# Weights that begin 16 bytes inside their tiles: a kernel whose matmuls run back to back, and the addresses they read

## The chip, the core and the metric

The kernel runs on one core of one Trainium2 chip. A core has five engines that run side by side and meet at semaphores: TensorE (PE in the profile, its weight loads PEld), VectorE (DVE), ScalarE (ACT), GpSimd (POOL) and SyncE (SP, which issues most DMAs here). The metric is device microseconds of one execution, the median of several runs.

## What is computed

Two transformer blocks on 256 tokens of width 1024, all in float32. The first has two layers (a sparse attention with compressed, selected and windowed keys; then a dilated attention), each followed by a SwiGLU feed-forward of 2816 hidden channels. The second has a feed-forward, a mixer of three branches (indexed sparse attention, a state-space scan, attention over a memory), and another feed-forward. There are so four feed-forwards:

```python
def swiglu(h, w_up, w_down):
    a, b = jnp.split(h @ w_up, 2, axis=-1)
    return (jax.nn.silu(a) * b) @ w_down
...
x = x + swiglu(rmsnorm(x, norm_ffn[layer]), ffn_w_up[layer], ffn_w_down[layer])
```

Most of the work is products of the activations with weight matrices that are read once from HBM.

## The kernel before

**Three products for one.** TensorE multiplies in a faster float32 form (F32R) that keeps fewer bits. So each operand is split into a rounded half h and the rest l, and a product is the sum of three: h with h, l with h, h with l. `mm3` (lines 223 to 230) issues them one after another into one PSUM bank: line 228 streams the activations' h against the weights' h, line 229 the activations' l against the weights' h, line 230 the activations' h against the weights' l. The activations move (128 partitions x 256 tokens), the weights are stationary (128x128). Every matmul has its own weight load.

**The path of a weight.** `load` (line 174) brings 128 x 2048 elements, 1 MB, into a `raw` tile by a DMA from SyncE's queue; `split` (line 181) makes of each 1024 columns a tile wh on ScalarE (line 187) and a tile wl on VectorE (line 188); four buffers of each. `units` (line 191) deals them out in pieces of 128 columns, 512 bytes. The activations are split the same way into tiles xh and xl in xs_pool (eight k-tiles, h and l, two buffers each), and the hidden channels of a feed-forward into hh and hl in a pool of its own.

**What sets the order.** A scheduler of the framework orders the instructions as it builds the program, by priorities and its own timeline. The projections take PSUM banks in turn (mm, sc, tr, ov: `take`, line 235). In a feed-forward the up projection is 44 units of eight k-tiles, 44 x 8 x 3 = 1056 matmuls in a row; the down projection follows with 8 units of 22 k-tiles of hidden channels, 528 matmuls.

**Where the tiles lie.** The pools are laid out in SBUF one after another, in bytes of each partition's row, tiles on multiples of 32: const, xres, a pad of 192, xs_pool (32 tiles of 1024 bytes), a pad of 320 (line 131), raw (4 x 8192), wsp (4 tiles wh and then 4 tiles wl, 4096 each), tmp (7360 bytes), then what a stage opens. So from the first tile of xs_pool to the first of the weights it is 32 x 1024 + 320 + 4 x 8192 = 65,856 bytes, which is 64 modulo 128 (320 modulo 512); all tiles and pieces in between are multiples of 512 bytes apart, so this holds for each pair of a piece of weights and a moving tile of xs_pool. From the first of the weights to the first hidden tile hh it is 8 x 4096 + 7360 + 4096 = 44,224 bytes in the first feed-forward; in the second 13,472 of a pool "late" and a pad of 320 come on top (58,016), in the third another 2112 (60,128), in the fourth the pad is 416 (58,112). Weights minus moving tile is thus 64, 96, 32 and 0 modulo 128 in the four down projections.

Of the kernel before, what the change touches and what calls it, by code (L numbers as in the profile page):

```python
# [12 lines left out]
F32R = mybir.dt.float32r  # L13
# [5 lines left out]
P = 128  # L19
# [102 lines left out]
class Builder:  # L122
    def __init__(self, ctx, tc, A):
        self.ctx, self.tc, self.nc, self.A = ctx, tc, tc.nc, A
        nc = self.nc
        e = ctx.enter_context
        self.cpool = e(tc.tile_pool(name="const", bufs=1))
        self.xpool = e(tc.tile_pool(name="xres", bufs=1))
        self.pad(e(tc.tile_pool(name="pad0", bufs=1)), 192)
        self.xs_pool = e(tc.tile_pool(name="xsplit", bufs=2))  # L130
        self.pad(e(tc.tile_pool(name="pad1", bufs=1)), 320)
        self.raw = e(tc.tile_pool(name="raw", bufs=4))
        self.wsp = e(tc.tile_pool(name="wsplit", bufs=4))
        self.tmp = e(tc.tile_pool(name="tmp", bufs=2))
        self.mm = e(tc.tile_pool(name="mm", bufs=2, space=PSUM))
        self.sc = e(tc.tile_pool(name="sc", bufs=2, space=PSUM))
        self.tr = e(tc.tile_pool(name="tr", bufs=2, space=PSUM))
        self.ov = e(tc.tile_pool(name="ov", bufs=2, space=PSUM))
        self.uid = 0
        self.turn = 0  # L140
        self.wide = True

        self.vec = self.cpool.tile([P, NVEC], F32, name="vec")
        self.gains = self.cpool.tile([P, KD * len(GAINS)], F32, name="gains")
        nc.scalar.dma_start(self.gains, A["vec"][:, :KD * len(GAINS)])
        self.con = self.cpool.tile([P, NCON], F32, name="con")
        self.ident = self.con[:, COFF["ident"]:COFF["ident"] + P]
        self.ones = self.cpool.tile([P, P], F32, name="ones")
        nc.vector.memset(self.ones, 1.0)
        self.mhalf = self.cpool.tile([P, 16], F32, name="mhalf")  # L150
        nc.gpsimd.memset(self.mhalf, -0.5)

        for _ in range(WARM):
            nc.tensor.matmul(self.bank("mm")[:, :P], self.ones, self.ones, start=True, stop=True)
# [25 lines left out]

    def split(self, v, kb, cols):
        nc = self.nc
        h = self.wsp.tile([P, 1024], F32R, tag="wh", name=self.n("wh"))
        l = self.wsp.tile([P, 1024], F32R, tag="wl", name=self.n("wl"))
        hv = h[:, :kb * cols].rearrange("p (k c) -> p k c", c=cols)
        lv = l[:, :kb * cols].rearrange("p (k c) -> p k c", c=cols)
        nc.scalar.activation(hv, v, AF.Copy)  # L187
        nc.vector.tensor_tensor(lv, v, hv.bitcast(F32), ALU.subtract)  # L188
        return [(hv[:, k], lv[:, k]) for k in range(kb)]
# [1243 lines left out]
```

## Time and profile before

| | |
|---|---|
| median of 3 runs | 1356.58 us (1354.99 to 1357.75) |
| profiled execution | 1361.28 us, its span 1359.3 us |
| TensorE busy | 1333.4 us, 98% of the span |
| VectorE busy | 999.9 us, 74% |
| ScalarE busy | 747.5 us, 55% |
| DMA queue of SyncE | 226 MB, 52.5% of the 16 engines' span |
| granted TensorE clock, mean | 0.995 |

The span is the time from the first to the last instruction of one profiled execution. Matmuls are pipelined: each is listed with about 0.28 us, but the next starts long before that is over, so the distance from start to start says how fast they go. In the view of busy time by stretch a row has the stretch and its length, then for PE, PEld, VectorE, ScalarE and GpSimd the busy time and, in brackets, the number of instructions that ran in the stretch, also those that had begun before it; then TensorE's granted clock (1.00 is full speed), the DMA engines' busy share and GB/s. The feed-forwards lie at about 170 to 346 us, 593 to 748, 798 to 949 and 1168 to 1346, the up projection first in each.

### The profile page before, as it was taken

How to read it: one execution, taken by the hardware profiler on the slowest of the kernel's cores; microseconds unless marked ns; L12 is line 12 of the kernel's file. 1: busy time of each engine (PE TensorE's matmuls, PEld its weight loads, DVE VectorE, ACT ScalarE, POOL GpSimd, SP SyncE). 2: the span in 40 equal slices, each digit the busy share in tenths (PEclk: the TensorE clock that was granted, in tenths of full speed). 3: DMA queues.
4: the chain of work that ended last, by engine and by line, in shares of the span. 5: the costliest groups of instructions: out<-in, count | busy, mean ns of one | idle time of the engine just before them, and what ended most of it. 6: DMA issues, size and time to landing. Idle time of an engine off the chain costs nothing.

```text
span 1359.3 us, 27471 instructions
## 1 busy us (share of the span) xinstructions
PE 1333.4 (98%) x10944; PEld 1266.8 (93%) x10944; DVE 999.9 (74%) x2087; ACT 747.5 (55%) x1414; POOL 188.7 (14%) x225
## 2 busy tenths in 40 slices
PE   8999999999999999999999999999999999999997
PEld 7786999999998887899999999999988879999997
DVE  6899677766697673998954877765699888777643
ACT  4677555545568785754544555544434665554442
POOL 4300100001210000422100310001032044000011
PEclk9999999999999999999999999999999999999998
DMA  9851365545865350456756466655754254655451
GB/s 280 251 160 63 109 198 188 188 142 188 247 202 182 114 139 9 147 191 216 233 182 201 154 207 201 194 187 157 243 162 148 79 170 158 199 186 189 152 193 43
DMA packets 227120, 232.77 MB, mean 171 GB/s; under 512 B 5944, under 2 KB 221184, under 8 KB 226992
## 3 DMA queue, kind: packets, MB, share of 16 engines
q1 hardware_dynamic: 223392, 226.14, 52.5%
q10 hardware_dynamic: 3600, 4.88, 1.0%
q8 instruction: 86, 1.41, 0.4%
q14 instruction: 42, 0.34, 0.1%
HBM read 226.69 MB, written 4.30 MB: 170 GB/s over the span
## 4 chain that ended last, share of the span: by engine, by line
PE 88%; DVE 6%; DMA 2%; issue 2%; ACT 1%; POOL 0%; SPq 0%; POOLq 0%; DVEq 0%; ACTq 0%
PE mm L228 11%; PE mm L229 11%; PE mm L230 11%; PE tr L230 6%; PE sc L230 6%; PE tr L228 6%; PE tr L229 6%; PE sc L228 6%; PE sc L229 6%; PE ov L473 3%; PE ov L228 3%; PE ov L230 3%; PE ov L229 3%; PE sc L777 2%; DVE wl L188 2%
## 5 line engine op out<-in xcount | busy, mean ns | idle before, releaser
L187 ACT ACTIVATE wh<-raw 128x1024 fp32r<-128x1024 f32 (+2 forms) x405 | 417.9, 1036 | 447.1 <-PE mm L229 141.7
L188 DVE TENSOR_TENSOR wl<-raw,wh 128x1024 fp32r<-128x1024 f32 (+2 forms) x405 | 489.9, 1212 | 167.9 <-ACT wh L187 163.1
L228 PE MATMUL mm<-xh,wh 128*128 128x256 f32 x952 | 272.5, 286 | 2.5 <-ACT wh L187 2.5
L230 PE MATMUL mm<-xh,wl 128*128 128x256 f32 x952 | 269.1, 283 | 1.0 <-DVE wl L188 1.0
L229 PE MATMUL mm<-xl,wh 128*128 128x256 f32 x952 | 269.4, 283 | 0.0
L228 PEld LDWEIGHTS mm<-xh,wh 128*128 128x128 f32 x952 | 180.8, 190 | 10.0 <-issue 4.7
L229 PEld LDWEIGHTS mm<-xl,wh 128*128 128x128 f32 x952 | 180.6, 190 | 4.3 <-issue 4.1
L230 PEld LDWEIGHTS mm<-xh,wl 128*128 128x128 f32 x952 | 179.8, 189 | 3.5 <-issue 1.6
L293 POOL TENSOR_TENSOR sqacc<-sqacc,sq 128x256 f32<-128x256 f32 x60 | 62.3, 1040 | 605.1 <-ACT sq L292 328.5
L228 PE MATMUL sc<-xh,wh 128*128 128x256 f32 x464 | 130.2, 281 | 1.8 <-ACT wh L187 1.8
L229 PE MATMUL sc<-xl,wh 128*128 128x256 f32 x464 | 130.0, 280 | 0.0
L230 PE MATMUL sc<-xh,wl 128*128 128x256 f32 x464 | 129.9, 280 | 0.0
L230 PE MATMUL tr<-xh,wl 128*128 128x256 f32 x440 | 123.2, 280 | 0.0
L229 PE MATMUL tr<-xl,wh 128*128 128x256 f32 x440 | 123.1, 280 | 0.0
L228 PE MATMUL tr<-xh,wh 128*128 128x256 f32 x440 | 123.1, 280 | 0.0
L228 PEld LDWEIGHTS sc<-xh,wh 128*128 128x128 f32 x464 | 88.0, 190 | 2.0 <-ACT wh L187 2.0
L229 PEld LDWEIGHTS sc<-xl,wh 128*128 128x128 f32 x464 | 87.6, 189 | 0.0
L230 PEld LDWEIGHTS sc<-xh,wl 128*128 128x128 f32 x464 | 87.2, 188 | 0.0
L228 PEld LDWEIGHTS tr<-xh,wh 128*128 128x128 f32 x440 | 83.4, 189 | 0.0
L229 PEld LDWEIGHTS tr<-xl,wh 128*128 128x128 f32 x440 | 83.0, 189 | 0.0
L230 PEld LDWEIGHTS tr<-xh,wl 128*128 128x128 f32 x440 | 82.7, 188 | 0.0
L228 PE MATMUL ov<-xh,wh 128*128 128x256 f32 x224 | 62.9, 281 | 0.0
(475 smaller groups left out, 3401.3 us busy)
## 6 DMA issues: line engine op xcount, KB each, us to landing
raw<-in_ffn_w_up_dram SPq DMA_DIRECT2D x44, 1024.0 KB, 5.3
raw<-in_ffn_w_in_dram SPq DMA_DIRECT2D x44, 1024.0 KB, 5.3
raw<-in_w_in_dram SPq DMA_DIRECT2D x17, 1024.0 KB, 5.2
raw<-in_ffn_w_down_dram SPq DMA_DIRECT2D x16, 1024.0 KB, 5.3
raw<-in_ffn_w_out_dram SPq DMA_DIRECT2D x16, 1024.0 KB, 5.3
raw<-in_b_w_q_dram SPq DMA_DIRECT2D x12, 1024.0 KB, 5.2
raw<-in_a_w_in_dram SPq DMA_DIRECT2D x8, 1024.0 KB, 8.7
bt<-u_scratch SPq DMA_DIRECT2D x28, 256.0 KB, 4.8
```

Source lines behind the costliest of these rows:

```text
L187: nc.scalar.activation(hv, v, AF.Copy)
L188: nc.vector.tensor_tensor(lv, v, hv.bitcast(F32), ALU.subtract)
L228: nc.tensor.matmul(ps, sh, mh, start=(i == 0), stop=False)
L229: nc.tensor.matmul(ps, sh, ml, start=False, stop=False)
L230: nc.tensor.matmul(ps, sl, mh, start=False, stop=(i == n - 1))
L293: nc.gpsimd.tensor_tensor(acc[:, 0], acc[:, 0], s, ALU.add)
L473: nc.tensor.matmul(O[64 * i:64 * i + 64, q0:q1], V[kb], pt[:, c0:c0 + q1 - q0], start=(start and kb == 0), stop=(stop and kb == 1), skip_g ...
L777: nc.tensor.matmul(ps, Q[d, h][:, qb * P:qb * P + P], K[d][g], start=(i == 0), stop=(i == 1))
```

## The change

Inside `split`, the tiles wh and wl become 1056 elements wide, and the kernel uses the elements 4 to 1027 of them, so that the weights begin 16 bytes inside the tile. The pad ahead of raw goes from 320 to 32 bytes. Nothing else changes: apart from that pad's memset, each engine has the same instructions in the same order.

```diff
-        self.pad(e(tc.tile_pool(name="pad1", bufs=1)), 320)
+        self.pad(e(tc.tile_pool(name="pad1", bufs=1)), 32)
...
     def split(self, v, kb, cols):
         nc = self.nc
-        h = self.wsp.tile([P, 1024], F32R, tag="wh", name=self.n("wh"))
-        l = self.wsp.tile([P, 1024], F32R, tag="wl", name=self.n("wl"))
+
+        h = self.wsp.tile([P, 1056], F32R, tag="wh", name=self.n("wh"))[:, 4:1028]
+        l = self.wsp.tile([P, 1056], F32R, tag="wl", name=self.n("wl"))[:, 4:1028]
         hv = h[:, :kb * cols].rearrange("p (k c) -> p k c", c=cols)
         lv = l[:, :kb * cols].rearrange("p (k c) -> p k c", c=cols)
```

From the first tile of xs_pool to the first weights it is now 32 x 1024 + 32 + 4 x 8192 + 16 = 65,584 bytes, 48 modulo 128. The buffers of a weight tile are 4224 bytes apart instead of 4096. The hidden tiles move with the pools: raw and the weights' tiles start 288 bytes lower, tmp and what follows 736 bytes higher.

## Rows read from the trace of the kernel before

**Rows 1.** Parts 1 and 4 of the page: busy us (share of the span) xinstructions; the chain.

```profile
PE 1333.4 (98%) x10944; PEld 1266.8 (93%) x10944; DVE 999.9 (74%) x2087; ACT 747.5 (55%) x1414; POOL 188.7 (14%) x225
...
PE 88%; DVE 6%; DMA 2%; issue 2%; ACT 1%; POOL 0%; SPq 0%; POOLq 0%; DVEq 0%; ACTq 0%
```

**Rows 2.** Busy time by stretch, all engines: stretch, length, busy us (xinstructions) per engine; clock.

```profile
180.00:280.00 100.00, 100.00 (x851) 100.00 (x850) 71.85 (x107) 50.40 (x71) 0.00 (x0) 1.00 0.56 183
292.00:342.00 50.00, 50.00 (x427) 50.00 (x426) 32.08 (x38) 25.30 (x37) 5.03 (x5) 1.00 0.60 198
600.00:685.00 85.00, 85.00 (x724) 85.00 (x723) 77.70 (x180) 43.06 (x62) 15.46 (x24) 1.00 0.69 220
692.00:745.00 53.00, 53.00 (x449) 53.00 (x448) 26.25 (x28) 22.54 (x28) 4.35 (x3) 1.00 0.62 203
802.00:882.00 80.00, 80.00 (x709) 80.00 (x708) 61.57 (x94) 43.52 (x63) 0.00 (x0) 1.00 0.61 194
892.00:942.00 50.00, 50.00 (x424) 50.00 (x424) 29.05 (x32) 23.19 (x32) 5.09 (x5) 1.00 0.58 188
1172.00:1282.00 110.00, 110.00 (x937) 110.00 (x936) 79.49 (x120) 56.30 (x82) 0.00 (x0) 1.00 0.58 190
1290.00:1340.00 50.00, 50.00 (x419) 50.00 (x419) 24.04 (x26) 20.49 (x25) 7.04 (x5) 1.00 0.46 149
```

**Rows 3.** Order of time, TensorE, second up projection: start us, length us, line, out<-in.

```profile
649.84 0.28 PE L228 MATMUL mm<-xh,wh 128*128 128x256 f32 x1
649.96 0.28 PE L229 MATMUL mm<-xl,wh 128*128 128x256 f32 x1
650.08 0.28 PE L230 MATMUL mm<-xh,wl 128*128 128x256 f32 x1
650.20 0.28 PE L228 MATMUL mm<-xh,wh 128*128 128x256 f32 x1
```

**Rows 4.** Order of time, TensorE, third up projection.

```profile
849.79 0.28 PE L228 MATMUL ov<-xh,wh 128*128 128x256 f32 x1
849.91 0.28 PE L229 MATMUL ov<-xl,wh 128*128 128x256 f32 x1
850.02 0.28 PE L230 MATMUL ov<-xh,wl 128*128 128x256 f32 x1
850.13 0.28 PE L228 MATMUL ov<-xh,wh 128*128 128x256 f32 x1
```

**Rows 5.** Order of time, the norm's sums ahead of the third up projection.

```profile
764.15 1.86 PEld L299 LDWEIGHTS ov<-ones,sqacc 128*128 128x128 f32 x16
...
764.26 1.84 PE L299 MATMUL ov<-ones,sqacc 128*128 128x1 f32 x16
```

**Rows 6.** Line 228's own matmuls by output bank: xcount, duration ns min/median/max, first and last start.

```profile
L228 PE MATMUL mm<-xh,wh x952: 276/281/684, 9.1 to 1282.5; 128*128 128x256 f32 x191
...
L228 PE MATMUL sc<-xh,wh x464: 276/281/385, 14.9 to 1285.3; 128*128 128x256 f32 x155
...
L228 PE MATMUL tr<-xh,wh x440: 276/281/364, 24.8 to 1276.8; 128*128 128x256 f32 x147
...
L228 PE MATMUL ov<-xh,wh x224: 276/281/369, 32.8 to 1279.6; 128*128 128x256 f32 x112
...
L228 PE MATMUL tr<-hh,wh x220: 277/281/365, 287.7 to 1348.9; 128*128 128x256 f32 x110
...
L228 PE MATMUL mm<-hh,wh x220: 277/281/285, 303.2 to 1332.8; 128*128 128x256 f32 x110
...
L228 PE MATMUL sc<-hh,wh x176: 277/281/285, 311.0 to 1340.7; 128*128 128x256 f32 x176
...
L228 PE MATMUL ov<-hh,wh x88: 277/281/285, 295.4 to 1324.9; 128*128 128x256 f32 x88
```

**Rows 7.** Part 5 of the page: the two instructions that split the weights.

```profile
L187 ACT ACTIVATE wh<-raw 128x1024 fp32r<-128x1024 f32 (+2 forms) x405 | 417.9, 1036 | 447.1 <-PE mm L229 141.7
L188 DVE TENSOR_TENSOR wl<-raw,wh 128x1024 fp32r<-128x1024 f32 (+2 forms) x405 | 489.9, 1212 | 167.9 <-ACT wh L187 163.1
```

## The prediction, on record before the changed kernel was run

> **What bounds the kernel now.** I read the busy shares first, then the chain of waits, then TensorE's busy time by stretch, then the order of time inside those stretches. TensorE is busy in 98% of the span and holds 88% of the chain that ended last [rows 1]; in the eight feed-forward stretches it is never idle and its granted clock is 1.00 [rows 2], which is the higher level, 2.4 GHz. So here time is the number of matmuls times the distance from the start of one to the start of the next. That distance is the thing to look at, because the change moves addresses only: no instruction is added, removed or moved on any engine; only the pad's memset shrinks.
>
> The reader should see in [rows 2] that the distance is not one number, though every row is of the same instruction, 256 moving columns against 128x128 weights. A matmul is listed for 0.281 us, so about 2.4 of the count in brackets were under way when the window opened. Without them: 100 us / 848.6 = 117.8 ns, 85 / 721.6 = 117.8 and 110 / 934.6 = 117.7 in three of the up projections, but 80 / 706.6 = 113.2 in the fourth. The down projections give 117.8, 118.7, 118.6 and 120.0, each to about 0.3. The single starts say the same: 0.11 to 0.12 apart in either, and over three matmuls 0.36 against 0.34 us [rows 3, 4].
>
> What differs is the address of the weights that are being loaded against that of the tile that is streaming: the load of the next weights runs beside every matmul. From the sizes in the section on the kernel, weights minus moving tile, modulo 128 bytes, is 64 for all the tiles of xs_pool and for the first down projection, 96 for the second, 32 for the third and 0 for the fourth. So the rows give a table: offset 0 costs 120.0 ns, 32 about 118.5, 96 about 118.7, and 64 either 117.8 or 113.2. At 64 there are two patterns at the very same addresses; a stream keeps the one it begins in until something interrupts it (the up projection of 802 to 882 us is in the fast one throughout, the other three in the slow one). Matmuls of one column, where nothing streams beside the load, show the floor that the load alone sets: 16 loads in 1.86 us, of which the last takes 0.19, so (1.86 - 0.19) / 15 = 111.3 ns apart [rows 5].
>
> **The change part by part.** The instructions that feel it: 2,080 x 3 = 6,240 matmuls with xh or xl moving and 704 x 3 = 2,112 with hh or hl [rows 6]; with the smaller tiles of the same pool (oh, oah, mgh, omh, ysh), which are not in those rows, 6,905 of the first kind. Going through their starts in the order of time, 6,725 of them follow one another without a stall, on average 116.5 ns apart: 2,019 (30%) at 113.3 and 4,706 at 117.8.
>
> (a) pad1 goes from 320 to 32 and the weights begin 16 bytes in: the offset of all xs_pool tiles goes from 64 to 48. No row shows an offset of 48, so I bound it. From above: the dearest row, 120.0, gives 6,725 x 3.5 ns = +23.5 us. From below: the load's own 111.3 gives 6,725 x 5.2 = -35 us; the fast pattern in every stream gives 6,725 x 3.2 = -21 us. The nearest rows are 32 (118.3 to 118.6) and the slow pattern of 64 (117.8); I take 118.1, between them: 6,725 x 1.6 = +11 us. This supposes that the fast pattern belongs to 64: it is seen at no other offset in [rows 2], though those are one long stream each, and at 64 three long streams of four miss it too.
>
> (b) The four down projections go from 64, 96, 32, 0 to 80, 112, 48, 16, because the weights' pool grows by 1,024 bytes ahead of them. Halfway values of the neighbouring rows are 118.2, 119.3, 118.1 and 119.2, against 117.8, 118.7, 118.5 and 120.0 now: +0.4, +0.6, -0.4 and -0.8 ns on some 527 each, which is 0 within 1 us. Bounds: all at 120.0 is +2.6 us, all at 113.3 is -11.5 us.
>
> (c) The tile of 1,056 instead of 1,024 elements moves the next buffer by 4,224 bytes, 33 x 128: the offset modulo 128 stays the same in all four buffers, modulo 512 it is now 48, 176, 304 and 432 where it was 320 in all. Whether the larger modulus counts no row shows, since slices of one weight tile lie 512 apart and buffers 4,096. I take nothing; if it did, some buffers would be good and some bad, and the mean lies inside the bounds of (a).
>
> (d) ScalarE and VectorE now write the halves 16 bytes off. Each piece takes them 1.04 and 1.21 us, 418 and 490 us in all [rows 7]. I take no change. The fullest stretch is 600 to 685 us, with VectorE busy 77.7 of 85 us [rows 2], so its splits there may cost some 7 us more before TensorE waits; elsewhere there is more room. DMA is 0.46 to 0.69 busy in these stretches and waits for no one, so raw's move by 288 bytes costs nothing.
>
> Sum: +11 + 0 + 0 + 0 = +11 us. The profiled execution took 1361.28 us (span 1359.3 and 2.0 around it), so it would take 1372.3. It lies 4.7 us above the median of the runs, which is about one long stream of 990 matmuls in the other pattern (990 x 4.5 ns = 4.5 us); runs of one kernel differ by such things. Off the median: 1356.58 + 11 = **1367.5 us**.
>
> **The rivals.**
>
> Faster: the fast pattern takes over. Place: the xs_pool streams, above all the three up projections of 800 to 1,000 matmuls that are slow now. For it: the pattern exists beside the slow one at 64, its matmuls are only 2 ns above the load's floor, and 48 is half as far from 64 as any other offset in the rows; against it: offsets 32 and 96, either side of 64, both cost over 118. It decides from the point where more than a third of the matmuls are in it: 118.1 less 4.8 ns times the share equals today's 116.5 at 0.33. In all streams it gives -21 us, with a little from the down projections 1334 us; at two thirds of them 1346.
>
> No change: the same two patterns in about the same shares (each 10% of the matmuls is worth 3.2 us), 1356.6 us. A mechanism that would do it is that addresses do not matter at all and the patterns are only a matter of how a stream begins; against it speaks that the last down projection is at 120.0 and the first at 117.8 with nothing else different. The Trainium skill has this as a rule: "TensorE: Matmul & The Clock Gate", in "Part 2: What happens when you issue a matmul", gives TensorE two independent SBUF read ports, one for the moving operand and one for weight loads, so that a load takes no read bandwidth from a running matmul. By that rule the sum would be 0; the rows disagree by 2.2 ns between two offsets, so I leave it a small share of this case.
>
> Much slower: 48 behaves as 0 does, 120.0 or more, +23.5 us and the down projections +2: 1382 us. For it only that the worst offset is as near to 32 as the best.
>
> **How the numbers follow.** Slow pattern alone (117.8 to 118.5): 0.39, with its own range from 1362 to 1373. Much slower: 0.08. No change: 0.15. Faster: 0.38. A difference of 0.2%, 2.7 us, is what a measurement can tell. Slower is 0.39 + 0.08 = 0.47, the same 0.15, faster 0.38. The range has to reach into both signs: down to 1331, just under the fast pattern in all streams (the load's floor, 1321, is left out), and up to 1376, which leaves out most of the much slower case.
>
> **What would show it.** In the changed kernel's stretches with no idle TensorE I would see the count fall to about 849 in 100 us of an up projection, in all four of them: right. A count of 883 in 100 us (113.3 ns) in two or more of them: the faster rival. Both kinds in the shares of now: no change. 833: the much slower one. The down projections show (b): the last should drop from 120.0 towards 119, the third stay within half a nanosecond. If VectorE's or ScalarE's mean per piece in [rows 7] rises by over a tenth, (d) was wrong, and TensorE would show waits for wl or wh in 600 to 685 us. What would make the forecast wrong is a fast pattern that is wider than the one offset where I can see it.

## The result, and the profile after

The changed kernel takes 1375.68 us (median of 4 runs, 1374.94 to 1375.89), the kernel before in the same measurement 1357.16 us (4 runs, 1354.99 to 1359.36). The ratio is 1.0129, with an interval of 1.0113 to 1.0145: slower by 18.5 us, where 11 were forecast. The profiled execution took 1374.94 us with a span of 1373.0 us.

First the page of the changed kernel, parts 1 and 4, beside [rows 1], and the two lines that answer to [rows 7]; line numbers in `split` and below it are one higher now.

```profile
PE 1350.4 (98%) x10944; PEld 1285.9 (94%) x10944; DVE 1000.4 (73%) x2087; ACT 748.2 (54%) x1414; POOL 186.8 (14%) x225
...
PE 94%; DVE 2%; issue 1%; DMA 1%; ACT 1%; SPq 0%; POOL 0%; POOLq 0%; DVEq 0%; ACTq 0%
...
L188 ACT ACTIVATE wh<-raw 128x1024 fp32r<-128x1024 f32 (+2 forms) x405 | 418.2, 1036 | 469.9 <-PE mm L230 146.2
L189 DVE TENSOR_TENSOR wl<-raw,wh 128x1024 fp32r<-128x1024 f32 (+2 forms) x405 | 491.1, 1215 | 167.4 <-ACT wh L188 161.0
```

VectorE and ScalarE do the same work in the same time (1036 ns a piece on one, 1215 against 1212 on the other). TensorE has the same 10,944 matmuls and is busy for 17.0 us more; its idle time in the span goes from 1359.3 - 1333.4 = 25.9 us to 1373.0 - 1350.4 = 22.6. So the two profiled spans are 17.0 - 3.3 = 13.7 us apart. The rest of the 18.5 us is in which executions were profiled: that of before lies 4.1 us above its median, that of the changed kernel 0.7 below.

Busy time by stretch in the changed kernel, the eight feed-forward stretches of [rows 2] (the columns as there; up and down projection in turn).

```profile
172.00:282.00 110.00, 110.00 (x934) 110.00 (x933) 79.88 (x120) 57.07 (x81) 0.00 (x0) 1.00 0.57 184
298.00:348.00 50.00, 50.00 (x427) 50.00 (x427) 33.08 (x40) 25.75 (x38) 6.05 (x6) 1.00 0.60 195
600.00:690.00 90.00, 90.00 (x748) 90.00 (x747) 81.04 (x189) 45.14 (x66) 15.80 (x25) 1.00 0.65 208
696.00:752.00 56.00, 56.00 (x473) 56.00 (x472) 26.85 (x29) 23.99 (x29) 4.34 (x3) 1.00 0.63 205
810.00:890.00 80.00, 80.00 (x670) 80.00 (x669) 58.47 (x90) 41.01 (x59) 0.00 (x0) 1.00 0.57 188
900.00:952.00 52.00, 52.00 (x442) 52.00 (x441) 31.38 (x35) 24.59 (x33) 5.11 (x5) 1.00 0.54 175
1185.00:1292.00 107.00, 107.00 (x892) 107.00 (x892) 76.02 (x114) 53.26 (x77) 0.00 (x0) 1.00 0.57 184
1300.00:1352.00 52.00, 52.00 (x442) 52.00 (x441) 25.74 (x29) 22.18 (x27) 7.02 (x5) 1.00 0.45 147
```

TensorE is never idle and its clock is 1.00 in all of them, as before. Taking off the same 2.4 of each count, the up projections go at 110 / 931.6 = 118.1 ns, 90 / 745.6 = 120.7, 80 / 667.6 = 119.8 and 107 / 889.6 = 120.3 from start to start. Before it was 117.8, 117.8, 113.2 and 117.7. The down projections are at 117.8, 119.0, 118.3 and 118.3.

A mean of 120.7 is no pattern of its own. TensorE in order of time in the second up projection shows two (start us, length us, line, out<-in); rows are left out, the first and last of each pattern stand.

```profile
650.08 0.29 PE L229 MATMUL ov<-xh,wh 128*128 128x256 f32 x1
650.21 0.28 PE L230 MATMUL ov<-xl,wh 128*128 128x256 f32 x1
650.32 0.29 PE L231 MATMUL ov<-xh,wl 128*128 128x256 f32 x1
650.45 0.28 PE L229 MATMUL ov<-xh,wh 128*128 128x256 f32 x1
650.57 0.29 PE L230 MATMUL ov<-xl,wh 128*128 128x256 f32 x1
650.70 0.28 PE L231 MATMUL ov<-xh,wl 128*128 128x256 f32 x1
...
652.30 0.29 PE L229 MATMUL ov<-xh,wh 128*128 128x256 f32 x1
...
653.02 0.28 PE L229 MATMUL mm<-xh,wh 128*128 128x256 f32 x1
653.14 0.28 PE L230 MATMUL mm<-xl,wh 128*128 128x256 f32 x1
...
655.15 0.28 PE L229 MATMUL mm<-xh,wh 128*128 128x256 f32 x1
```

From 650.08 to 652.30 there are 18 matmuls: 2.22 / 18 = 123.3 ns, and the starts step by 0.13 and by 0.11 or 0.12 in turn. From 653.02 to 655.15 there are 18 again: 2.13 / 18 = 118.3 ns. Between the two the weights' buffer changes, and with it the output bank. The bank does not make the difference: the pieces of 24 matmuls go on alternating, and bank mm has both, 118.0 ns from 652.7 us and 123.4 in its next piece, from 661.3 us. With buffers 4,224 bytes apart, 4,224 being 128 modulo 256, the offset (address of the weights minus address of the moving tile) is 48 in one buffer and 176 in the next, modulo 256. Modulo 128, as the prediction counted, both are 48.

Over the whole program, by their starts: the xs_pool matmuls that follow one another without a stall, some 6,720 in each kernel, went from 116.48 to 119.19 ns on average, 6,720 x 2.71 ns = +18.2 us; the 2,105 of the down projections from 118.7 to 118.3, -0.8 us.

### The profile page after: what moved, and what is told of

Same layout as the page of the kernel before. It is cut to its first block, busy times and chain, and to the rows that moved or that the text cites. A ratio compares the mean times of both kernels' runs of the same rounds, so it can differ in the third digit from the quotient of the medians.

```text
span 1373.0 us, 27471 instructions
## 1 busy us (share of the span) xinstructions
PE 1350.4 (98%) x10944; PEld 1285.9 (94%) x10944; DVE 1000.4 (73%) x2087; ACT 748.2 (54%) x1414; POOL 186.8 (14%) x225
## 4 chain that ended last, share of the span: by engine, by line
PE 94%; DVE 2%; issue 1%; DMA 1%; ACT 1%; SPq 0%; POOL 0%; POOLq 0%; DVEq 0%; ACTq 0%
PE mm L229 12%; PE mm L230 12%; PE mm L231 12%; PE sc L229 6%; PE sc L231 6%; PE tr L231 6%; PE tr L229 6%; PE sc L230 6%; PE tr L230 6%; PE ov L474 3%; PE ov L229 3%; PE ov L231 3%; PE ov L230 3%; PE sc L778 2%; PE tr L452 1%
## 5 line engine op out<-in xcount | busy, mean ns | idle before, releaser
L188 ACT ACTIVATE wh<-raw 128x1024 fp32r<-128x1024 f32 (+2 forms) x405 | 418.2, 1036 | 469.9 <-PE mm L230 146.2
L189 DVE TENSOR_TENSOR wl<-raw,wh 128x1024 fp32r<-128x1024 f32 (+2 forms) x405 | 491.1, 1215 | 167.4 <-ACT wh L188 161.0
```

## The experiments

All numbers in bytes are offsets of the weights against the moving tile. "Mean distance" is from start to start, of the matmuls that follow one another without a stall. A "stream" is one projection. A "pattern" is a sequence of distances that a stream repeats; at some offsets there are several, and which one a stream falls into when it begins is called its draw.

**One part alone: the wider tiles.** Weights from byte 0, but tiles of 1056 elements, so that the offset goes 64, 192, 64, 192 with the buffer.

```diff
-        self.pad(e(tc.tile_pool(name="pad1", bufs=1)), 320)
+        self.pad(e(tc.tile_pool(name="pad1", bufs=1)), 64)
...
-        h = self.wsp.tile([P, 1024], F32R, tag="wh", name=self.n("wh"))
-        l = self.wsp.tile([P, 1024], F32R, tag="wl", name=self.n("wl"))
+        h = self.wsp.tile([P, 1056], F32R, tag="wh", name=self.n("wh"))
+        l = self.wsp.tile([P, 1056], F32R, tag="wl", name=self.n("wl"))
```

> Tiles of 1056 elements as in the changed kernel, but the weights begin at the tile's start; the pad is 64, so the weights minus the xs_pool tiles are 64 and 192 modulo 256 in turn (both 64 modulo 128). Theory 1 (the distance from start to start is set by weights minus moving tile modulo 256, and what costs in the changed kernel is that half its buffers are at 48): 64 keeps its two patterns (113.3 and 117.8 ns); 192 is not seen yet, so 1350 to 1372 us, and each class has its own distance in the trace. Rival A (the start off the 32-byte grid costs by itself): the time of before, 1357 us within 4. Rival B (what costs is that the offset changes from buffer to buffer, which breaks the fast pattern): no distances of 113.3 in streams of over 60 matmuls, about 117.8 everywhere, 1366 us or more.

Measured: 1344.01 us (4 runs, 1343.12 to 1344.79), ratio 0.9905 (0.9886 to 0.9924). The wider tile, far from costing anything, gains 13 us. None of the three expectations had this time: it lies 6 us below the least that Theory 1 gave, and rivals A and B expected 1357 and 1366 us. The first feed-forward stream, in order of time, around one change of buffer:

```profile
177.26 0.28 PE L228 MATMUL sc<-xh,wh 128*128 128x256 f32 x1
...
178.32 0.28 PE L228 MATMUL sc<-xh,wh 128*128 128x256 f32 x1
...
179.36 0.28 PE L228 MATMUL tr<-xh,wh 128*128 128x256 f32 x1
...
180.38 0.28 PE L228 MATMUL tr<-xh,wh 128*128 128x256 f32 x1
```

Nine matmuls take 1.06 us up to 178.32 (117.8 ns) and 1.02 us from 179.36 (113.3 ns). The buffer changes at 178.9, from offset 192 to 64. This stream began at 117.8 in both offsets, fell into 113.3 there, and stayed at 113.3 through each later change of buffer to its end. The other up projections do the same within their first few buffers, or begin in it; the second leaves it at a stall near 650 us, when TensorE waits, and is back in it from 659 us on. About three quarters of the xs_pool distances are in the fast pattern, against 30% before, and they average 114.5 ns. The first down projection, at 64 and 192 too, is at 113.3 throughout.

**The other part alone: the 16 bytes, without the alternation.** The two halves share one tile of 2112 elements, 8,448 bytes or 33 x 256, so that the offset is one number throughout: 48, then 176, and 64 with the weights at byte 0 as the control. The pad is 32, 160 and 64, and s is 0 in the control. The shared tile changes the order of some instructions in the mixer.

```diff
-        self.pad(e(tc.tile_pool(name="pad1", bufs=1)), 320)
+        self.pad(e(tc.tile_pool(name="pad1", bufs=1)), 32)
...
-        h = self.wsp.tile([P, 1024], F32R, tag="wh", name=self.n("wh"))
-        l = self.wsp.tile([P, 1024], F32R, tag="wl", name=self.n("wl"))
+        s = 4
+        t = self.wsp.tile([P, 2112], F32R, tag="wh", name=self.n("wh"))
+        h, l = t[:, s:s + 1024], t[:, s + 1024:s + 2048]
```

> Both halves in one tile of 2112 elements (8448 bytes, 33 x 256), weights begin 16 bytes in, pad 32: all buffers at 48 modulo 256. Theory 1: the pattern of 117 and 130 ns in all buffers, a mean of 120 to 123.4 for xs_pool tiles, so 6,800 x (3.5 to 7) ns = 24 to 47 us over before: 1381 to 1404 us. Rival A: as the changed kernel, 1375 us within 4. Rival B: less than the changed kernel, about 1366 us, and one constant pattern.

> As the run with all buffers at 48, but the pad is 160, so all are at 176 modulo 256 (48 modulo 128 again). Theory 1: 118.1 ns for xs_pool tiles and no 130: 6,800 x 1.6 = 11 us over before, 1368 us. Rival A: 1375 us within 4. Rival B: about 1366 us, the same as with all at 48. If modulo 128 is all that counts, the runs with 48 and 176 agree within 0.3%.

> Control for the two runs with one tile for both halves: the same tile, weights at its start, pad 64, so all xs_pool offsets are 64 modulo 256 as before (64 modulo 512 where it was 320). All theories: the time of before, 1357 us within 5, with both patterns, 113.3 and 117.8. If it differs, the one tile or the offset modulo 512 has an effect of its own.

Measured: 48 gives 1376.08 us, ratio 1.014 (1.0113 to 1.0167); 176 gives 1367.38 us, 1.0077 (1.0061 to 1.0092); the control at 64 gives 1352.3 us, 0.996 (0.9945 to 0.9976). Busy time by stretch at 48, first and fourth up projection:

```profile
175.00:280.00 105.00, 105.00 (x894) 105.00 (x893) 76.16 (x114) 52.20 (x78) 0.00 (x0) 1.00 0.56 185
1185.00:1292.00 107.00, 107.00 (x870) 107.00 (x869) 73.54 (x109) 49.26 (x72) 0.00 (x0) 1.00 0.54 178
```

The same at 176:

```profile
175.00:280.00 105.00, 105.00 (x891) 105.00 (x891) 75.89 (x115) 51.73 (x78) 0.00 (x0) 1.00 0.57 186
...
1185.00:1285.00 100.00, 100.00 (x849) 100.00 (x848) 71.80 (x108) 48.17 (x71) 0.00 (x0) 1.00 0.56 183
```

At 48 one stream goes at 105 / 891.6 = 117.8 ns and another, at the very same offset, at 107 / 867.6 = 123.3; the two between them are at 117.8 and 118.3. At 176 there is one pattern: 118.2 and 118.1. So the offset of 48 has three patterns, and a stream keeps the one it began in. Theory 1's 1368 us for 176 came true, its 1381 to 1404 for 48 did not: one up projection of four fell into the dear pattern of 123.3, and not all. Rival A's 1375 us fits 48 alone and fails at 176, which starts off the 32-byte grid as well; rival B's equal times for both fail by 8.7 us. The control is 4.9 us faster than before. In the profiled executions, whose spans are 8.8 us apart, the draws are worth 4.1 us of this (about 43% of its xs_pool distances are fast, against 30%), and 0.7 us is in the second down projection; the rest is not in these distances and stays open. Its means are those of the kernel before at the same offset (113.3 or 117.8 at 64, 118.3 at 32, 120.0 at 0), but for the second down projection at 96: 117.3 against 118.7.

**Measuring the disputed cost by itself.** The start inside the shared tile is set for each half of each projection, so that one run shows eight offsets (XS holds a pair of starts for each up projection, shifts a pair for each down projection).

```diff
+        s = self.shift // 4
...
+                self.shift = XS[mp > 4]
...
+            self.shift = shifts[mp > 1]
```

> A measurement of the disputed cost by itself: one tile for both halves with a start that the kernel sets by stage, so that the first 20 and the last 24 units of each up projection, and the first and second half of each down projection, run at offsets of their own: up projections 0, 32; 96, 128; 160, 192; 224, 64, down projections 64, 192; 128, 224; 96, 160; 0, 32, all modulo 256. Its total time means nothing. Theory 1 with modulus 128: 0 and 128 cost 120.0 ns, 32 and 160 about 118.3, 96 and 224 about 118.7, 64 and 192 either 113.3 or 117.8. With modulus 256: 0 to 96 as those, 128 to 224 may differ. Rival A: all of these within 1 ns of 117.8 or 113.3, as none starts off the 32-byte grid.

> The same with the offsets between: up projections 48, 16; 80, 112; 144, 176; 208, 240, down projections 208, 240; 48, 176; 16, 144; 80, 112. Theory 1: 48 at 118 to 123.4 ns with 130s, 176 at 118.1 without; 80, 112 and 16 near the means of the changed kernel's down projections (117.7, 119.1, 118.2, which mixed two classes each). Rival A: all alike, above 118.5, whatever the offset.

One execution each: 1360.39 and 1366.4 us. Busy time by stretch with multiples of 32: offsets 0, 128, 192 and 64.

```profile
176.00:220.00 44.00, 44.00 (x369) 44.00 (x368) 31.46 (x49) 21.75 (x33) 0.00 (x0) 1.00 0.59 192
...
688.00:715.00 27.00, 27.00 (x230) 27.00 (x229) 13.74 (x15) 11.77 (x16) 2.88 (x2) 1.00 0.65 215
...
826.00:886.00 60.00, 60.00 (x512) 60.00 (x511) 42.78 (x64) 29.07 (x43) 0.00 (x0) 1.00 0.59 193
...
1222.00:1280.00 58.00, 58.00 (x515) 58.00 (x514) 43.31 (x64) 28.68 (x42) 0.00 (x0) 1.00 0.62 201
```

With odd multiples of 16: offsets 48, 16 and 176.

```profile
176.00:221.00 45.00, 45.00 (x368) 45.00 (x367) 31.82 (x49) 21.47 (x34) 0.00 (x0) 1.00 0.57 188
227.00:287.00 60.00, 60.00 (x510) 60.00 (x509) 42.69 (x63) 29.05 (x43) 0.00 (x0) 1.00 0.57 190
...
831.00:891.00 60.00, 60.00 (x510) 60.00 (x509) 42.65 (x64) 29.18 (x43) 0.00 (x0) 1.00 0.59 190
```

In the order of the lines: 44 / 366.6 = 120.0 ns, 118.6, 117.7 and 113.1; then 123.1, 118.2 and 118.2. The mean distances of the long streams in all the runs told of here, or of their pieces where the offset turns, by offset modulo 256:

| offset | ns | offset | ns |
|---|---|---|---|
| 0 | 119.8 to 120.0 | 16 | 118.3 to 118.5 |
| 32 | 118.3 | 48 | 117.8, 118.3 or 123.1 to 123.3 |
| 64 | 113.3 or 117.8 | 80 | 118.5 to 118.8 |
| 96 | 117.3 to 118.8 | 112 | 119.4 to 120.0 |
| 128 | 118.4 to 118.7 | 144 | 116.7, 119.6 or 120.0 |
| 160 | 120.0 | 176 | 118.1 to 118.3 |
| 192 | 113.3 or 117.8 | 208 | 116.7 |
| 224 | 116.7 | 240 | 117.3 to 120.1 |

0 and 128, 16 and 144, 48 and 176, 96 and 224 differ: the modulus is at least 256. So Theory 1 with modulus 128 fails, and so does rival A, which expected nearly equal costs within either run. It is the difference of the two addresses that counts, and not the weights' address by itself: in the kernel before the weights' tiles stay where they are and the hidden tiles move, and 0 costs 120.0 and 32 costs 118.3; in the run with multiples of 32 the weights move past fixed xs_pool tiles, and 0 costs 120.0 and 32 costs 118.4. And being an odd multiple of 16 is no cost by itself: those go from 116.7 (208) to 123.3 (48), the others from 113.3 (64) to 120.0 (0). But 113.3 was seen at none of them. Theory 1's 117.7 and 119.1 for 80 and 112, taken from means of two offsets, were low by about 1 ns. What the change gave up is 64, where all xs_pool matmuls lay before, and with it the fast pattern.

**Does a theory drawn from this foretell a time?** All moving tiles, hidden ones too, at 64 and 192 in turn; and all at 64 throughout. Both change the pads ahead of the hidden tiles (the third feed-forward's goes from 320 to 288); the first has the wide tiles besides.

```diff
-                b.ffn(xs, "norm_ffn1", A["ffn_w_up1"], A["ffn_w_down1"], 1.0, lambda: b.mem_norm(late), skew=320)
+                b.ffn(xs, "norm_ffn1", A["ffn_w_up1"], A["ffn_w_down1"], 1.0, lambda: b.mem_norm(late), skew=352)
...
-                b.ffn(xs, "ffn2_norm_2", A["ffn2_w_in_2"], A["ffn2_w_out_2"], 0.5, skew=416)
+                b.ffn(xs, "ffn2_norm_2", A["ffn2_w_in_2"], A["ffn2_w_out_2"], 0.5, skew=352)
```

> The wide weight tiles of the run with 64 and 192 in turn (width 1056, weights from byte 0), and besides the three skews before the down projections of the second, third and fourth feed-forward changed (320 to 352, 320 to 288, 416 to 352 bytes), so that every moving tile of the large projections, up and down, lies 64 or 192 bytes past its weights modulo 256. Theory 1 (each offset modulo 256 has a few possible mean distances, a stream keeps one until the offset changes, a change between 64 and 192 draws again, and 113.3 ns once drawn stays): the three down projections of 528 matmuls each go from 117.2, 119.1 and 119.1 ns to 113.4, some 2 + 3 + 3 = 8 us less than the run with wide tiles, near 1336 us, 1332 to 1342. Theory 2 (113.3 in the wide run was a matter of each stream's start and not of the offsets): the downs stay at 117 to 119, near 1344 us, and the up streams may fall back to 117.8, near 1352 us.

> The kernel before with the same three changed skews, so that every moving tile of the large projections, up and down, lies 64 bytes past its weights modulo 256, all through (width 1024, weights from byte 0): no turn between 64 and 192. Theory 1 (a stream at a constant offset keeps the mean distance that it has drawn): each up stream is at 113.3 or at 117.8 ns from start to end; the downs are at 113.3 or 117.8; 1357 less up to 8 us for the downs, and some 10 to 15 us more or less for the draws, near 1350 us, 1340 to 1360. Theory 2 (the offset alone decides, and 64 is as good as 64 and 192 in turn): the same time as the kernel with both, near 1336 to 1344 us.

Measured: 64 and 192 in turn 1335.33 us (4 runs, 1334.55 to 1337.67), ratio 0.9832 (0.9818 to 0.9846); 64 throughout 1351.87 us (5 runs, 1349.56 to 1353.4), 0.9944 (0.993 to 0.9958). Both lie within 2 us of the first theory's number, and some 8 us or more from the second's. The page, and busy time by stretch, of 64 and 192 in turn:

```profile
PE 1307.3 (98%) x10944; PEld 1240.7 (93%) x10944; DVE 999.7 (75%) x2087; ACT 747.5 (56%) x1414; POOL 188.0 (14%) x225
...
PE 83%; DVE 10%; DMA 2%; issue 2%; ACT 1%; POOL 0%; SPq 0%; POOLq 0%; DVEq 0%; ACTq 0%
```

```profile
175.00:275.00 100.00, 100.00 (x884) 100.00 (x883) 75.24 (x112) 51.95 (x75) 0.00 (x0) 1.00 0.60 196
290.00:335.00 45.00, 45.00 (x399) 45.00 (x398) 30.20 (x36) 24.47 (x36) 5.04 (x5) 1.00 0.59 194
595.00:670.00 75.00, 74.41 (x654) 74.01 (x653) 70.68 (x168) 38.24 (x57) 15.06 (x23) 1.00 0.68 221
680.00:735.00 55.00, 55.00 (x488) 55.00 (x487) 28.38 (x31) 24.28 (x29) 4.36 (x3) 1.00 0.65 212
...
1266.00:1316.00 50.00, 50.00 (x443) 50.00 (x442) 25.44 (x27) 21.56 (x26) 7.06 (x5) 1.00 0.46 153
```

And of 64 throughout, first and second feed-forward:

```profile
175.00:280.00 105.00, 105.00 (x894) 105.00 (x893) 76.38 (x115) 53.37 (x77) 0.00 (x0) 1.00 0.58 189
292.00:342.00 50.00, 50.00 (x427) 50.00 (x427) 32.16 (x38) 25.30 (x37) 5.03 (x5) 1.00 0.60 197
600.00:685.00 85.00, 84.60 (x740) 84.12 (x740) 78.97 (x183) 43.83 (x64) 15.50 (x24) 1.00 0.68 220
690.00:740.00 50.00, 50.00 (x444) 50.00 (x443) 25.62 (x27) 22.58 (x28) 4.37 (x3) 1.00 0.62 206
```

With the turns every down projection goes at 113.3 by its starts (here 55 / 485.6 = 113.3, 50 / 440.6 = 113.5). Without them a feed-forward keeps what it drew as long as nothing interrupts it: the first is at 117.8 up and down (105 / 891.6, 50 / 424.6), the second for the most part at 113.3 by its starts (50 / 441.6 = 113.2 in the down projection). The second up projection has three stalls, and they change its pattern, at one and the same offset (order of time; rows are left out):

```profile
655.25 0.28 PE L228 MATMUL tr<-xh,wh 128*128 128x256 f32 x1
...
655.59 0.28 PE L228 MATMUL mm<-xh,wh 128*128 128x256 f32 x1
...
655.86 0.39 PE L230 MATMUL mm<-xh,wl 128*128 128x256 f32 x1
656.08 0.28 PE L228 MATMUL mm<-xh,wh 128*128 128x256 f32 x1
...
658.55 0.28 PE L228 MATMUL sc<-xh,wh 128*128 128x256 f32 x1
...
662.45 0.38 PE L230 MATMUL tr<-xh,wl 128*128 128x256 f32 x1 [0.30 <-DVE wl L188]
...
663.03 0.28 PE L228 MATMUL tr<-xh,wh 128*128 128x256 f32 x1
...
663.37 0.28 PE L228 MATMUL tr<-xh,wh 128*128 128x256 f32 x1
```

Three matmuls take 0.34 us before 655.59 (113.3 ns), 21 take 2.47 us from 656.08 (117.6 ns), and three take 0.34 us again after the wait for wl at 662.45. So a stall can change the pattern either way. In a stream that nothing interrupts it is the change of offset that lets it leave the slow pattern, and the offset decides which patterns there are. In the faster kernel TensorE is idle for 0.6 of 75 us in the second up projection, with VectorE busy for 70.7, and VectorE's share of the chain has gone from 6% [rows 1] to 10%: the next limit may be near there, which no run tests.

## Why the prediction was right in direction and short in size

What bounds the kernel was read rightly: the same matmuls, never idle, and the time moves with the distance between starts. TensorE's busy time carries all of the difference between the two profiles.

The time, 1375.68 us, lies only 0.3 us inside the range, which ended at 1376. That it lies inside is partly luck: the runs with all weights at 48 go up to 1379.03 us.

(a) is the step that was mis-sized: 118.1 ns for the new offset, +11 us. In half of the buffers, at 176, it holds to a few tenths of a ns, and where all lie at 176 the time is 1367.38 us, next to the forecast's 1367.5. In the other half, at 48, three of the four up projections fell into a pattern of 123.1 ns that no row of the kernel before shows. The mean is then +2.7 ns on 6,720 matmuls, +18 us, instead of +1.6 ns and +11 us. It stays inside the upper bound of (a), 120.0, but single streams leave that bound: it had been taken as the dearest row, and the dearest row was not the dearest pattern. Of the sign that the prediction set for being right, about 849 matmuls in 100 us in all four up projections, only the first shows it (934 in 110 us).

(c) is where it could have been seen: "whether the larger modulus counts no row shows ... I take nothing". It counts: modulo 256 a buffer's step of 4,224 bytes is 128, so every other buffer lies at 176 and not at 48. The runs in which the offset turns suggest why this matters beyond the mean of good and bad buffers: each change of offset gives the stream another start, and it moves on until it meets a pattern that survives the turns. At 64 and 192 that pattern is the fast one (113.3 in both). At 48 and 176 it is the dear one: in the changed kernel's third up projection 48 is at 117.8 or 118.3 in its first buffers, at 123.1 from 833 us, and at nothing else until the end; the fourth does the same from 1205 us, and the second has it from its first buffers. In the first, where the offset changes after 48 matmuls and not after 24, it never came. In the third down projection, 48 and 176 as well, 123.3 came in one piece of 24 matmuls at 48, and after the next piece, 18 matmuls at 176, it was gone. So the dear pattern stayed in three of these five streams, and that the turns select it is a reading, not shown.

(b) was right, 0 within 1 us (-0.8), and the last down projection did fall from 120.0, to 118.2. Its working was partly luck: the means hide two offsets each, 208 at 116.7 and 80 at 118.7 in the first.

(d) was right: 1036 and 1215 ns, and no new wait for wh or wl in the feed-forwards.

Three readings of the prediction need a word. Its 6,905 matmuls of the first kind do not follow from the names: line 228 has 2,080 with xh and 272 with the smaller tiles moving, and three times 2,352 is 7,056; the sum uses the 6,725 distances, which hold. It leaves out 288 matmuls, too few to matter, in which the weights move and xh or xl is loaded. And its floor of 111.3 ns comes from matmuls of plain float32, each of which stands in the trace as four loads and four matmuls (16 for the four that line 299 issues); no row has F32R loads without a stream beside them.

Of the rivals, "faster" asked for a fast pattern wider than 64; 48 and 176 have none. "No change" supposed that addresses do not matter; a run with nothing but the width of the weight tile and a pad changed gained 0.95%. The Trainium skill's rule behind that rival ("TensorE: Matmul & The Clock Gate", "Part 2: What happens when you issue a matmul": independent read ports, so that a load takes no read bandwidth from a running matmul) would give 0 us here. The runs give 113.3 to 123.3 ns for the same matmul, by its addresses and the pattern that it falls into, so the measurement decides against a cost of 0, though no run shows where the time goes. "Much slower" had the right fear at the wrong place: 48 does not behave as 0, it has a worse pattern of its own, in half of the buffers; the mark set for it, 833 matmuls in 100 us, is about what the second, third and fourth up projection show (748 in 90 us, 670 in 80 us, 892 in 107 us).

Not settled: why an offset has several patterns, and why the fast one survives the turn between 64 and 192 and the dear one that between 48 and 176. Steps finer than 16 bytes were not tried, nor a kernel with 192 throughout, nor turns between other pairs.

## What to carry to other kernels

Where matmuls with their own weight loads run back to back, look at the distance from start to start by stream before anything else, and set it against the difference of the two operands' addresses, modulo 256 at least and for each buffer by itself: here that alone moves the kernel by 3%, from 1335 to 1376 us, with no instruction changed but the pads' memsets. A mean between two known distances is a mixture until the single starts say otherwise. And a pool's buffer step is part of the layout: a step that is no multiple of 256 puts neighbouring buffers at different offsets.

## What the runs showed that was not expected

The same matmul at the same addresses has up to three steady distances (117.8, 118.3 and 123.3 ns at 48), each kept for 800 to 1,000 matmuls. A step between two buffers with different offsets lets a stream leave one without a stall. In the kernel with both projections at 64 and 192 in turn, the ten longest runs of matmuls without a stall (180 to 993 matmuls: the feed-forwards' projections, the second up projection in two pieces, and one in the mixer) all end in 113.3 ns; of the same ten at 64 throughout five stay at 117.8. These ten are fewer draws than that, as each down projection goes on in the pattern of the up projection ahead of it. And some shorter runs do not leave the slow pattern even with the turns: 91 matmuls at 150 to 161 us and 72 at 377 to 386 us stay at 117.8. The fast pattern is 2 ns above the 111.3 of the plain float32 loads [rows 5].
